# Norms on the tokens' partitions: sums of squares and the spreading of roots by transposes instead of fp32 products

## The chip, the core and the metric

The program runs on one core of a Trainium2 chip. A core has a matrix engine (TensorE, in the profile PE, with its weight loads as PEld), a vector engine (VectorE, DVE), an activation engine (ScalarE, ACT), a general engine (GpSimd, POOL) and a queue engine for transfers (SyncE, SP). Each engine has its own queue and takes its instructions in order; semaphores let one wait for another. SBUF and PSUM have 128 partitions; TensorE writes to PSUM only. A matrix instruction takes a stationary operand (128 x up to 128, loaded first) and a moving one, and gives stationary transposed times moving.

The metric is the time of one execution on the device in microseconds, as the median of several runs.

## The reference, cut to what matters

A two-layer encoder step: layer 0 is a state-space (SSD) mixer and a gated feed-forward net, layer 1 is banded attention and a second feed-forward net. There are 1088 tokens (1024 of a prompt, 64 of a running stream) of width 1024. Every part is wrapped in norms:

```python
def rmsnorm(x, w):
    xf = x.astype(jnp.float32)
    y = xf * lax.rsqrt(jnp.mean(xf * xf, axis=-1, keepdims=True) + EPS)
    return (y * w.astype(jnp.float32)).astype(x.dtype)
...
        xp = xp + rmsnorm(mp, nw[1])
        xp = xp + rmsnorm(swiglu(rmsnorm(xp, nw[2]), ffn_w_in[layer], ffn_w_out[layer]), nw[3])
```

and the SSD mixer has a gated norm of its own over four groups of 512 columns:

```python
    y = y.reshape(b, L, D_INNER) * jax.nn.silu(z.astype(jnp.float32))
    yg = y.reshape(b, L, SSM_GROUPS, D_INNER // SSM_GROUPS)
    yg = yg * lax.rsqrt(jnp.mean(yg * yg, axis=-1, keepdims=True) + EPS)
```

What matters here: per token one sum of squares over the features, one reciprocal root, and a product of every feature with that root.

## The kernel before, in words

**Layout.** Activations lie transposed: features on the partitions, tokens along the free axis. A token's sum of squares therefore runs over partitions and over feature tiles. Tokens come in three slices of 384, 384 and 320 (`SL`), or in four quarters of 256, 256, 288 and 288 (`QS`).

**A norm.** `add_sq` (lines 475 to 481) squares feature tiles on ScalarE and adds them up on GpSimd or VectorE into a tile `ssum` of 128 partitions by tokens. `rstd` (483) takes the sum over partitions: for each block of 128 tokens TensorE multiplies the block of `ssum` (stationary) with a column of ones (line 489), so a block's 128 sums arrive as one column of a PSUM tile `nst`, tokens on the partitions. Nine small VectorE operations (493 to 504) turn up to three such columns into reciprocal roots, one factor short: the constant `RL` is left for later. `diag` (506) makes, on VectorE, a diagonal matrix of the roots out of the identity, and `bcast` (513) multiplies a full matrix `frac`, all of whose entries are `RL`, with it on TensorE (516): the result, in a PSUM tile `nbp`, has on every partition the row of all tokens' roots. ScalarE copies it to SBUF (520), and VectorE uses it as a row factor.

**Where norms stand.** `rb_steps` (523) strings these together for the three norms at the start (`start_norm`), the two norms of each quarter after each mixer (`chain`, both layers), the end norm of each slice after each feed-forward net (`end`), and the scale for keys and values (also in `end`). The very last norm, of slice 2 in layer 1, has a second sum `more` with the squares of the last feature tile. The SSD stage calls `rstd` alone, once for each of four groups and three slices (`ssd_task`, line 931), and keeps the roots in `rst`; `build_y` (584) later spreads them, 16 times, and scales y with them on its way from DRAM to the output projection.

**Products.** The large products run as three reduced-precision products of high and low parts (lines 455 to 457, 1271 to 1273, 1470 to 1472); the products of the norms are full fp32 ones. Transposes through TensorE with the identity are in use elsewhere, as for B (799), x (830) and the attention weights (1715).

**Order.** TensorE's order is written out by hand: the program is one long run of large products, and side work (norms, SSD blocks, attention blocks) is held in generators. A counter `st.t` estimates TensorE's time; a generator yields `cost, delay, condition`, and is resumed at the next pump once the counter has moved on by the delay and the condition holds. So `RB_WAIT`, `CHW` and the other tables of delays say how much later on TensorE's queue a broadcast stands than the sums it needs. The order on the other engines is made by a planner at build time from priorities (`tc.high_priority`) and from when tiles come free. Two PSUM buffers (`ax`) are shared by `nst`, `nbp` and the small products and transposes of the side work; the ring `DG` holds two diagonals at most, and `DG.free` is a condition for the next one. Weights and scratch data come in on SP's queue.

Of the kernel before, what the change touches and what calls it, by code (L numbers as in the profile page):

```python
# [8 lines left out]
F32 = mybir.dt.float32  # L9
F32R = mybir.dt.float32r  # L10
I32 = mybir.dt.int32
AF = mybir.ActivationFunctionType
# [42 lines left out]
RWP = 3000, 0, 0  # L55

KBUF = 5
DGB = 2
RAWB, HLB, SGB = 2, 3, 5
NR, NRX = 16, 13  # L60

# [312 lines left out]
def hybrid_kernel(  # L374
# [21 lines left out]
    make_identity(nc, ident)  # L396
    ones = cp.tile([P, P], F32, name="ones")
    G.memset(ones, 1.0)
    frac = cp.tile([P, P], F32, name="frac")
    G.memset(frac, RL)  # L400
    pcs = cp.tile([P, NPC], F32, name="pcs")
    A.activation(ones[:, 0:1], ones[:, 0:1], AF.Square)

# [19 lines left out]
    W.tc, W.lent = tc, Lent(RX)  # L423
    W.raws.append(W.lent)
    UC = Cells(384, (R, 99))
    DG = Ring(nsb, "dg", DGB, [P, 3, P])

    def v4(t, n):
        return t[:, :4 * n].rearrange("p (k n) -> p k n", k=4)
# [52 lines left out]

    def rstd(ssum, inv, r, nb, more=None):

        sp, ts = ax("nst"), [ssum] if more is None else [ssum, more]
        for j, t in enumerate(ts):
            for i in range(nb):
                c = 4 * j + i
                PE.matmul(sp[:, c:c + 1], t[:, i * P:(i + 1) * P], ones[:, 0:1], start=True, stop=True)
        with tc.high_priority(HIP):  # L490
            v = nsb.tile([P, 12], F32, tag="nv", bufs=2, name="nv")
            a, h, y = v[:, 0:nb], v[:, 4:4 + nb], v[:, 8:8 + nb]
            V.tensor_scalar(a, sp[:, :nb], inv, EPS, op0=ALU.mult, op1=ALU.add)
            if more is not None:
                V.scalar_tensor_tensor(a, sp[:, 4:4 + nb], inv, a, op0=ALU.mult, op1=ALU.add)
            V.tensor_scalar(y.bitcast(I32), a.bitcast(I32), -0.5, float(0x5F3759DF), op0=ALU.mult, op1=ALU.add)


            V.tensor_tensor(h, y, y, op=ALU.mult)
            V.tensor_tensor(h, h, a, op=ALU.mult)  # L500
            V.scalar_tensor_tensor(a, h, RP[0], h, op0=ALU.add, op1=ALU.mult)
            V.scalar_tensor_tensor(a, a, RP[1], h, op0=ALU.add, op1=ALU.mult)
            V.scalar_tensor_tensor(a, a, RP[2], h, op0=ALU.add, op1=ALU.mult)
            V.scalar_tensor_tensor(r, a, RP[3], y, op0=ALU.add, op1=ALU.mult)

    def diag(r3, nb):
        dg = DG.get()
        V.tensor_tensor(
            dg[:, :nb], ident.unsqueeze(1).to_broadcast([P, nb, P]), r3.unsqueeze(2).to_broadcast([P, nb, P]), op=ALU.mult
        )  # L510
        return dg

    def bcast(dg, a, n, rb=None):

        bp = ax("nbp")
        PE.matmul(bp[:, :n], frac, dg.rearrange("p a b -> p (a b)")[:, a:a + n], start=True, stop=True)
        DG.put()
        if rb is None:
            rb = nsb.tile([P, 384], F32, tag="rb", bufs=1, name="rb")
        A.copy(rb[:, :n], bp[:, :n])  # L520
        return rb[:, :n]

    def rb_steps(ssum, n, out, wait=None, rb=None, more=None):

        nb = (n + P - 1) // P
        nr = nsb.tile([P, 4], F32, tag="nr", bufs=2, name="nr")
        rstd(ssum, 1.0 / D, nr[:, :nb], nb, more)
        yield 0.2, 0, DG.free
        with tc.high_priority(HIP):
            dg = diag(nr[:, :nb], nb)  # L530
        yield 0.1, wait or RB_WAIT
        with tc.high_priority(HIP):
            out.append(bcast(dg, 0, n, rb))
        yield 0.5, 0

    def apply_split(src, rb, wcol, n, dh, dl, eng=0):
        f = nsb.tile([P, 384], F32, tag="sq", bufs=2, name="uf")
# [46 lines left out]
    def build_y():  # L584

        for q, half in ((0, 0), (1, 0), (0, 1), (1, 1), (2, 0), (3, 0), (2, 1), (3, 1)):
            o, n = QS[q]
            got = []
            c0, c1, a = ((0, 2, 0), (2, 4, 0), (4, 7, 0), (6, 9, 32))[q]
            for kh in range(2):  # L590
                g = 2 * half + kh
                yield 0, 0, lambda: R.free(2) and DG.free() and all((g, s) in rst_done for s in ((0,), (0, 1), (1, 2), (2,))[q])
                h, l_ = rr(v4(R.get(), n)), rr(v4(R.get(), n))
                dg = diag(rst[:, c0:c1, g], c1 - c0)
                yield 0, 4.0
                rb = bcast(dg, a, n)
                with tc.high_priority(BYP[q]):
                    for k in range(4):
                        t_ = stage[0]()[:, :n]
                        nc.sync.dma_start(t_, yd_[:, 4 * g + k, o:o + n])  # L600
                        V.scalar_tensor_tensor(t_, t_, col(C_GN + 4 * g + k), rb, op0=ALU.mult, op1=ALU.mult)
                        A.copy(h[:, k, :], t_)
                        V.tensor_tensor(l_[:, k, :], t_, h[:, k, :], op=ALU.subtract)
                        got.append((h[:, k, :], l_[:, k, :]))
                yield 0.5, 0
            uy[half][q] = got
# [705 lines left out]
    def back(layer, start, cpost, xsrc, xmid, cpre, cpost2, xout, rb_out, done2):  # L1312
# [3 lines left out]
        with ExitStack() as es:  # L1316
# [30 lines left out]
            def end(s, y, ss, more=None):  # L1347

                o, n = SL[s]
                if s not in xss:  # L1350
                    yield from end_load(s)
                xs, xc = xss.pop(s)
                out = []
                if s == 2 and more is None:
                    yield 0, EP_W[2]
                steps = rb_steps(ss, n, out, ER_W[s], more=more)
                if more is not None:

                    xps = {}

                    def hold(ms):
                        for m in ms:
                            xps[m] = mm("xp") if m > 3 else px.tile([P, 512], F32, tag="mm", name="xp")
                            PE.matmul(xps[m][:, :n], ident, xs[m][0], start=True, stop=False)

                    yield next(steps)
                    hold(range(4))
                    yield next(steps)
                    yield next(steps)
                    hold((4, 5))  # L1370
                    for m in range(KD):
                        ym = y[:, m, :n]
                        V.scalar_tensor_tensor(ym, ym, col(cpost2 + m), out[0], op0=ALU.mult, op1=ALU.mult)
                        if m in xps:
                            PE.matmul(xps[m][:, :n], ident, ym, start=False, stop=True)
                            A.copy(ym, xps[m][:, :n])
                        else:
                            V.tensor_tensor(ym, ym, xs[m][0], op=ALU.add)
                        nc.sync.dma_start(xout[:, m, o:o + n], ym)
                    for c in xs:  # L1380
                        xc.put(c)
                    yr.put()
                    return
                yield from steps
                for m in range(KD):
                    ym = y[:, m, :n]
                    with tc.high_priority(ENP[s]):
                        V.scalar_tensor_tensor(ym, ym, col(cpost2 + m), out[0], op0=ALU.mult, op1=ALU.mult)
                        V.tensor_tensor(ym, ym, xs[m][0], op=ALU.add)
                        if m % 2:  # L1390
                            nc.sync.dma_start(xout[:, m - 1:m + 1, o:o + n], y[:, m - 1:m + 1, :n])
                    yield 0, ES[s]
                for c in xs:
                    xc.put(c)
# [598 lines left out]
```

## Time and profile before

| | |
|---|---|
| time of three runs | 3015.92, 3015.95, 3016.99 us; median 3015.95 |
| span of the profiled execution, first to last instruction | 3019.2 us; the page gives no other time for it |
| granted TensorE clock, mean | 0.995 |
| instructions | 56662 |
| moved by DMA | 335.43 MB, mean 111 GB/s |

In the profile, a group line gives the line of the kernel, the engine, the operation, output and inputs by the program's names, shapes, count, busy time and mean duration, then the engine's idle time before it and what ended it. A timeline line gives start and duration in us, and in brackets the idle time before it and what ended that. Durations of TensorE instructions overlap, since they are pipelined: what one costs the queue is the distance from start to start. A window line gives the stretch, the busy time of each engine, the granted TensorE clock and the DMA's share and rate.

### The profile page before, as it was taken

Reading aid. Unit: us, or ns where it says so; the run is one execution under the profiler, and the core shown is the slowest. Engines: PE = TensorE matmul, PEld = TensorE weight load, DVE = VectorE, ACT = ScalarE, POOL = GpSimd, SP = SyncE. Lnnn points to the kernel's source line nnn. Section 1 sums busy time; section 2 is a strip of 40 time slices with the busy share of each in tenths; the row PEclk is TensorE's granted clock in tenths of the full one; section 3 lists DMA queues with packets and bytes.
Section 4 is the critical chain, followed back from the end, with each engine's and each line's share of the span. In section 5 each row is a group of like instructions: output and inputs, shape, how many; then the busy total and the mean of one; then the engine's idle time right before and its main releaser. Section 6 shows DMA issues by size and latency. Waiting matters only on the chain.

```text
span 3019.2 us, 56662 instructions
## 1 busy us (share of the span) xinstructions
PE 2971.5 (98%) x21803; PEld 2907.2 (96%) x21803; DVE 2047.7 (68%) x4517; ACT 1462.0 (48%) x2643; POOL 699.4 (23%) x849
## 2 busy tenths in 40 slices
PE   8999999999999999999999999999999999999999
PEld 7999999998999999999999899999999999999998
DVE  7778877785768545575546878777768655475544
ACT  6756566564443322244444666555653322244443
POOL 1333333330121334351101000000131343452111
PEclk9999999999999999999999999999999999999999
DMA  3111111124555222245655322222356222245654
GB/s 120 34 58 52 59 48 51 60 67 139 182 143 157 74 80 75 80 151 179 200 168 164 96 81 79 70 64 84 118 173 180 74 77 81 79 146 176 212 177 135
DMA packets 180671, 335.43 MB, mean 111 GB/s; under 512 B 18192, under 2 KB 128400, under 8 KB 180400
## 3 DMA queue, kind: packets, MB, share of 16 engines
q1 hardware_dynamic: 178608, 325.45, 34.5%
q0 software_dynamic: 1792, 6.36, 1.1%
q8 instruction: 171, 2.80, 0.4%
q14 instruction: 100, 0.82, 0.1%
HBM read 264.69 MB, written 62.60 MB: 108 GB/s over the span
## 4 chain that ended last, share of the span: by engine, by line
PE 85%; DVE 8%; ACT 2%; DMA 2%; issue 2%; POOL 0%; SPq 0%; DVEq 0%; ACTq 0%; POOLq 0%
PE px L1271 9%; PE px L1272 9%; PE px L1273 9%; PE mm L455 7%; PE mm L457 7%; PE mm L456 7%; PE po L1470 6%; PE po L1471 6%; PE po L1472 6%; PE mmx L455 3%; PE mmx L456 3%; PE mmx L457 3%; PE po L1754 2%; PE ptp L1715 1%; PE yp L896 1%
## 5 line engine op out<-in xcount | busy, mean ns | idle before, releaser
L455 PE MATMUL mm<-r,hl 128*128 128x384 f32 (+2 forms) x1664 | 554.9, 333 | 8.6 <-DVE dt L705 4.1
L457 PE MATMUL mm<-r,hl 128*128 128x384 f32 (+2 forms) x1664 | 540.4, 325 | 1.6 <-DVE hl L352 0.9
L456 PE MATMUL mm<-r,hl 128*128 128x384 f32 (+2 forms) x1664 | 539.4, 324 | 0.0
L340 DVE TENSOR_TENSOR hl<-raw,hl 128x1024 fp32r<-128x1024 f32 (+1 forms) x219 | 263.0, 1201 | 222.1 <-ACT hl L339 219.3
L1272 PE MATMUL px<-r,hl 128*128 128x288 f32 (+1 forms) x1184 | 348.1, 294 | 0.0
L455 PEld LDWEIGHTS mm<-r,hl 128*128 128x128 f32 x1664 | 315.8, 190 | 11.8 <-ACT BT L782 4.3
L457 PEld LDWEIGHTS mm<-r,hl 128*128 128x128 f32 x1664 | 314.9, 189 | 3.3 <-DVE hl L352 2.3
L456 PEld LDWEIGHTS mm<-r,hl 128*128 128x128 f32 x1664 | 315.7, 190 | 0.5 <-issue 0.2
L1271 PE MATMUL px<-r,hl 128*128 128x288 f32 x1056 | 311.3, 295 | 0.0
L1273 PE MATMUL px<-r,hl 128*128 128x288 f32 x1056 | 311.3, 295 | 0.0
L339 ACT CAST hl<-raw 128x1024 fp32r<-128x1024 f32 (+1 forms) x219 | 219.1, 1005 | 179.5 <-PE po L1472 102.9
L481 POOL TENSOR_TENSOR ssum<-ssum,sq 128x256 f32<-128x256 f32 (+3 forms) x97 | 128.0, 1320 | 656.3 <-ACT sq L480 643.1
L1272 PEld LDWEIGHTS px<-r,hl 128*128 128x128 f32 x1184 | 222.7, 188 | 0.0
L1273 PE MATMUL px<-rx,hl 128*128 128x256 f32 x768 | 215.9, 281 | 5.1 <-DVE hl L340 5.1
L1271 PE MATMUL px<-rx,hl 128*128 128x256 f32 x768 | 216.5, 282 | 0.7 <-ACT hl L339 0.7
L1471 PE MATMUL po<-rx,hl 128*128 128x384 f32 (+1 forms) x624 | 202.0, 324 | 0.4 <-DVE rx L1335 0.3
L1470 PE MATMUL po<-rx,hl 128*128 128x384 f32 (+1 forms) x608 | 198.6, 327 | 0.6 <-ACT rx L1334 0.6
L1271 PEld LDWEIGHTS px<-r,hl 128*128 128x128 f32 x1056 | 198.6, 188 | 0.4 <-DVE u L1286 0.3
L1273 PEld LDWEIGHTS px<-r,hl 128*128 128x128 f32 x1056 | 198.6, 188 | 0.0
L1472 PE MATMUL po<-rx,hl 128*128 128x384 f32 (+1 forms) x608 | 196.9, 324 | 0.0
L1272 PE MATMUL px<-rx,hl 128*128 128x256 f32 x640 | 179.6, 281 | 0.0
L289 POOL TENSOR_TENSOR tt<-raw 128x512 f32<-128x512 f32 x40 | 54.8, 1369 | 449.5 <-DMA raw<-in_w_f_dram 311.6
(364 smaller groups left out, 8197.6 us busy)
## 6 DMA issues: line engine op xcount, KB each, us to landing
raw<-in_w_f_dram SPq DMA_DIRECT2D x154, 512.0 KB, 3.7
rx<-in_w_f_dram SPq DMA_DIRECT2D x54, 512.0 KB, 3.7
raw<-in_w_in_dram SPq DMA_DIRECT2D x40, 512.0 KB, 3.6
sg<-hscr SPq DMA_DIRECT2D x88, 192.0 KB, 3.6
raw<-in_w_f_dram SPq DMA_DIRECT2D x44, 384.0 KB, 3.3
raw<-in_w_so_dram SPq DMA_DIRECT2D x32, 512.0 KB, 3.8
raw<-in_w_kv_dram SPq DMA_DIRECT2D x18, 512.0 KB, 3.6
raw<-in_w_o_dram SPq DMA_DIRECT2D x16, 512.0 KB, 3.7
```

The costliest lines, as they stand in the source:

```text
L339: self.nc.scalar.copy(h, v)
L340: (eng or self.eng or self.nc.vector).tensor_tensor(lo, v, h, op=ALU.subtract)
L455: PE.matmul(ps[:, :n], h_, xh, start=(first and i == 0), stop=False)
L456: PE.matmul(ps[:, :n], h_, xl, start=False, stop=False)
L457: PE.matmul(ps[:, :n], l_, xh, start=False, stop=(last and i == nk - 1))
L481: (eng or G).tensor_tensor(ssum[:, :n], ssum[:, :n], q[:, :n], op=ALU.add)
L1271: PE.matmul(ps, wh, ah[:, k, :], start=(k == 0), stop=False)
L1272: PE.matmul(ps, wh, al[:, k, :], start=False, stop=False)
L1273: PE.matmul(ps, wl, ah[:, k, :], start=False, stop=(k == 3))
L1470: PE.matmul(ps[:, :n], wh, xh, start=(k == 0), stop=False)
L1471: PE.matmul(ps[:, :n], wh, xl, start=False, stop=False)
L1472: PE.matmul(ps[:, :n], wl, xh, start=False, stop=(k == FT - 1))
```

## The change

The sums of squares: where there is one sum tile (all norms but the last), each block of 128 tokens of `ssum` is transposed with the identity into `nst`, and VectorE sums the 128 columns of each block (`tensor_reduce`), then scales by the mean's factor. The last norm keeps its products.

The spreading: `diag`, its ring and `frac` go. `bcast` takes the column of roots of a block, repeated 128 times, as the stationary operand of a transpose with the identity; the result has the block's roots as a row on every partition. The factor `RL` moves to the scale of ScalarE's copy. For `build_y` the transposes cover whole blocks from the first one on, and the copy takes the wanted columns.

The delays: `rb_steps` has two yields instead of three (costs 0.3 and 0.35 in place of 0.2, 0.1 and 0.5) and no condition on a diagonal; `build_y` waits 2.5 in place of 4.0 before its broadcast; the end of the last slice is written for two yields.

```diff
-    frac = cp.tile([P, P], F32, name="frac")
-    G.memset(frac, RL)
...
-    DG = Ring(nsb, "dg", DGB, [P, 3, P])
...
-        sp, ts = ax("nst"), [ssum] if more is None else [ssum, more]
-        for j, t in enumerate(ts):
+        sp = ax("nst")
+        if more is None:
             for i in range(nb):
-                c = 4 * j + i
-                PE.matmul(sp[:, c:c + 1], t[:, i * P:(i + 1) * P], ones[:, 0:1], start=True, stop=True)
+                PE.transpose(sp[:, i * P:(i + 1) * P], ssum[:, i * P:(i + 1) * P], ident)
+        else:
+            for j, t in enumerate((ssum, more)):
+                for i in range(nb):
+                    c = 4 * j + i
+                    PE.matmul(sp[:, c:c + 1], t[:, i * P:(i + 1) * P], ones[:, 0:1], start=True, stop=True)
...
-            V.tensor_scalar(a, sp[:, :nb], inv, EPS, op0=ALU.mult, op1=ALU.add)
-            if more is not None:
+            if more is None:
+                sums = sp[:, :nb * P].rearrange("p (a b) -> p a b", b=P)
+                V.tensor_reduce(a, sums, axis=mybir.AxisListType.X, op=ALU.add)
+                V.tensor_scalar(a, a, inv, EPS, op0=ALU.mult, op1=ALU.add)
+            else:
+                V.tensor_scalar(a, sp[:, :nb], inv, EPS, op0=ALU.mult, op1=ALU.add)
...
-    def diag(r3, nb):
-        dg = DG.get()
-        V.tensor_tensor(
-            dg[:, :nb], ident.unsqueeze(1).to_broadcast([P, nb, P]), r3.unsqueeze(2).to_broadcast([P, nb, P]), op=ALU.mult
-        )
-        return dg
-
-    def bcast(dg, a, n, rb=None):
+    def bcast(r, a, n, rb=None):
 
         bp = ax("nbp")
-        PE.matmul(bp[:, :n], frac, dg.rearrange("p a b -> p (a b)")[:, a:a + n], start=True, stop=True)
-        DG.put()
+        for i in range((a + n + P - 1) // P):
+            PE.transpose(bp[:, i * P:(i + 1) * P], r[:, i:i + 1].to_broadcast([P, P]), ident)
...
-        A.copy(rb[:, :n], bp[:, :n])
+        A.activation(rb[:, :n], bp[:, a:a + n], AF.Copy, scale=RL)
...
-        yield 0.2, 0, DG.free
+        yield 0.3, wait or RB_WAIT
         with tc.high_priority(HIP):
-            dg = diag(nr[:, :nb], nb)
-        yield 0.1, wait or RB_WAIT
-        with tc.high_priority(HIP):
-            out.append(bcast(dg, 0, n, rb))
-        yield 0.5, 0
+            out.append(bcast(nr, 0, n, rb))
+        yield 0.35, 0
...
-                dg = diag(rst[:, c0:c1, g], c1 - c0)
-                yield 0, 4.0
-                rb = bcast(dg, a, n)
+                yield 0, 2.5
+                rb = bcast(rst[:, c0:c1, g], a, n)
...
-                    yield next(steps)
+                    got = next(steps)
                     hold(range(4))
-                    yield next(steps)
+                    yield got
                     yield next(steps)
```

More of the change, by code (lines that the diff above doesn't have):

```diff
@@ L57 @@
 KBUF = 5
-DGB = 2
 RAWB, HLB, SGB = 2, 3, 5
@@ L591, in build_y @@
                 g = 2 * half + kh
-                yield 0, 0, lambda: R.free(2) and DG.free() and all((g, s) in rst_done for s in ((0,), (0, 1), (1, 2), (2,))[q])
+                yield 0, 0, lambda: R.free(2) and all((g, s) in rst_done for s in ((0,), (0, 1), (1, 2), (2,))[q])
                 h, l_ = rr(v4(R.get(), n)), rr(v4(R.get(), n))
-                dg = diag(rst[:, c0:c1, g], c1 - c0)
-                yield 0, 4.0
-                rb = bcast(dg, a, n)
+                yield 0, 2.5
+                rb = bcast(rst[:, c0:c1, g], a, n)
                 with tc.high_priority(BYP[q]):
```

## The prediction

> **What bounds the kernel now.** I read the page first, then the windows, then the timeline around the norms.
>
> ```profile
> PE 2971.5 (98%) x21803; PEld 2907.2 (96%) x21803; DVE 2047.7 (68%) x4517; ACT 1462.0 (48%) x2643; POOL 699.4 (23%) x849
> ...
> PE 85%; DVE 8%; ACT 2%; DMA 2%; issue 2%; POOL 0%; SPq 0%; DVEq 0%; ACTq 0%; POOLq 0%
> ```
>
> TensorE (PE) is busy 98% of the span and the chain that ended last runs through it for 85%. That is an average, so two windows show the extremes (us; then busy time of PE, PEld, DVE, ACT, POOL; granted clock; DMA share; GB/s).
>
> ```profile
> 130.00:640.00 510.00, 509.92 (x3567) 494.54 (x3566) 408.93 (x1062) 313.12 (x491) 171.40 (x323) 1.00 0.17 53
> 640.00:705.00 65.00, 59.64 (x430) 56.47 (x429) 56.80 (x159) 39.05 (x76) 15.69 (x18) 0.97 0.33 101
> ```
>
> From 130 to 640 us (the SSD stage) PE has no idle time: a nanosecond saved on its queue is saved in the end. From 640 to 705 us, where the last SSD blocks, the gated y and the output projection meet, PE idles 5.4 us and VectorE (DVE) is busy 87%: there DVE decides. So I price PE's queue everywhere, then take off the places where PE waits for DVE anyway.
>
> **Sums of squares: products out, transposes in.** Which rows belong to the norms (instruction counts; ns minimum/median/maximum; first and last start):
>
> ```profile
> L489 PE MATMUL nst<-ones,ssum x158: 164/250/271, 21.4 to 3006.6; 128*128 128x1 f32 x158
> L489 PE MATMUL nst<-ones,ssg x72: 165/250/252, 229.0 to 690.7; 128*128 128x1 f32 x72
> L516 PE MATMUL nbp<-dg,frac x88: 377/405/799, 30.7 to 3009.7; 128*128 128x256 f32 x32, 128*128 128x288 f32 x32, 128*128 128x384 f32 x16, 128*128 128x320 f32 x8
> ```
>
> An fp32 product is two instructions: 230 are 115 products, in 40 norms; 88 are 44 broadcasts. Durations overlap, so what a group costs PE's queue is read from start to start:
>
> ```profile
> 899.57 0.28 PE L457 MATMUL mmx<-rx,hl 128*128 128x256 f32 x1
> 899.69 0.72 PE L489 MATMUL nst<-ones,ssum 128*128 128x1 f32 x6
> 900.27 0.36 PE L455 MATMUL mmx<-rx,hl 128*128 128x256 f32 x1
> ```
>
> ```profile
> 797.09 0.50 PE L489 MATMUL nst<-ones,ssum 128*128 128x1 f32 x4
> 797.45 0.38 PE L455 MATMUL mmx<-r,hx 128*128 128x288 f32 x1
> ```
>
> Three blocks take 0.58 us (900.27 less 899.69), two take 0.36. The replacement is in the kernel already, as the transposes of B into `bnp`: one instruction a block, since the three blocks show x3, not x6.
>
> ```profile
> 221.04 0.49 PE L799 MATMUL bnp<-ident,BT 128*128 128x128 f32 x3
> 221.29 0.42 PE L455 MATMUL mm<-r,hl 128*128 128x384 f32 x1
> ```
>
> Three transposes take 0.25 us. Two have no clean row; I take two thirds, 0.17, between 0.08 and 0.25. From the code, 31 norms have three blocks (3 at the start, 12 SSD groups, 8 of the chains, 5 ends, 3 for the K/V scale), 8 chain norms have two, and the last norm (the one with a second sum) keeps its products. Saved: 31 x (0.58 - 0.25) = 10.2 us and 8 x (0.36 - 0.17) = 1.5 us.
>
> **Broadcast: product out, transposes in.** The old cost by width:
>
> ```profile
> 1487.53 0.81 PE L516 MATMUL nbp<-dg,frac 128*128 128x384 f32 x2
> 1487.88 0.63 PE L1470 MATMUL po<-rx,hl 128*128 128x384 f32 x1
> ```
>
> ```profile
> 1652.59 0.70 PE L516 MATMUL nbp<-dg,frac 128*128 128x320 f32 x2
> 1652.89 0.57 PE L455 MATMUL mm<-r,hl 128*128 128x384 f32 x1
> ```
>
> ```profile
> 908.05 0.65 PE L516 MATMUL nbp<-dg,frac 128*128 128x288 f32 x2
> 908.32 0.50 PE L455 MATMUL mmx<-rx,hl 128*128 128x256 f32 x1
> ```
>
> ```profile
> 662.05 0.59 PE L516 MATMUL nbp<-dg,frac 128*128 128x256 f32 x2
> 662.29 0.52 PE L455 MATMUL mm<-r,hl 128*128 128x384 f32 x1
> ```
>
> Against 0.25 for three transposes (0.17 for two at width 256): 8 x 0.10 (384) + 4 x 0.05 (320) + 16 x 0.02 (288) + 16 x 0.07 (256) = 2.4 us. Together PE's queue gets 14.1 us shorter. If two blocks cost 0.25 or 0.08, the 24 two-block groups move this by about 2 us either way. The stationary operand here is one column repeated 128 times, which no transpose of the trace has. The nearest loads:
>
> ```profile
> L830 PEld LDWEIGHTS xtp<-ident,xsT 128*128 128x128 f32 x144 | 17.7, 141 | 0.7 <-POOL xsT L783 0.2
> L847 PEld LDWEIGHTS bcp<-acr,sel 128*128 128x128 f32 x96 | 14.8, 191 | 4.2 <-ACT ea L856 4.2
> ```
>
> `sel` is a repeated column too, in a product, and loads in 191 ns against 141 for a transpose; products with plain weights load in 190, so the repetition looks free and I take no charge. The bound: 50 ns on each of 116 such transposes (16 x 2 + 28 x 3), 5.8 us. Below, no gain.
>
> **VectorE.** It loses `diag` and gains the sum. The sum has no row; the nearest is a PSUM read of the same size. The view of groups (busy us, mean ns):
>
> ```profile
> L508 DVE TENSOR_TENSOR dg<-ident,nr 128x384 f32<-128x384 f32 x20 | 11.2, 558 | 0.5
> L800 DVE COPY Bn<-bnp 128x384 f32<-128x384 f32 x12 | 6.6, 552 | 0.8 <-PE bnp L799 0.7
> ```
>
> I take 0.55 us, with 0.4 below (the scan alone, estimated as the 552 less the 160 of a three-element operation of the norm) and 1.1 above, twice the copy; at 1.1 the chains at the five norms where PE waits (two at 41, one each at 682, 1684 and 2238) would be 0.55 longer each, 2.7 us less gain. So at 0.55 a norm followed by its broadcast stays as long on DVE: 0.55 earlier, 0.56 less later. The scaling on ScalarE's copy costs nothing: the copy exists already, and only a factor is added. [...]
>
> **Where PE waits, and the rest of the sum.** Near 41-46 us two start norms share DVE and PE stands until their roots are there; near 682-700 DVE decides.
>
> ```profile
> 46.33 2.26 PE L516 MATMUL nbp<-dg,frac 128*128 128x384 f32 x4 [2.31 <-DVE nr L504]
> ```
>
> ```profile
> 682.09 1.47 PE L489 MATMUL nst<-ones,ssg 128*128 128x1 f32 x12 [1.33 <-DVE ssg L928]
> ...
> 682.93 0.16 DVE L493 TENSOR_SCALAR nv<-nst 128x3 f32<-128x3 f32 x1
> ```
>
> Lost there: two start norms and their broadcasts (0.9), the three norms at 682-690 and the six narrow broadcasts at 662-700 (1.4), and the broadcasts at 1653-1690 and 2221-2253 (0.4): 2.7 us. The norms of the last two places keep their saving, because the DVE chain starts when the shorter PE group ends and is no longer than before; the sum waits for PE where the scaling of the old sums did, so the same work queues behind it on DVE, only 0.55 us longer. In the 640-705 stage DVE drops six diagonals, first and last
>
> ```profile
> 663.07 0.41 DVE L508 TENSOR_TENSOR dg<-ident,rst 128x256 f32<-128x256 f32 x1
> ...
> 700.71 0.43 DVE L508 TENSOR_TENSOR dg<-ident,rst 128x256 f32<-128x256 f32 x1 [1.84 <-PE nbp L516]
> ```
>
> (6 x 0.42 = 2.5) and takes three sums (1.65): 0.9 us back. The tail has no cover at all:
>
> ```profile
> 3008.51 0.16 DVE L504 SCALAR_TENSOR_TENSOR nr<-nv 128x3 f32<-128x3 f32 x1
> 3008.70 0.56 DVE L508 TENSOR_TENSOR dg<-ident,nr 128x384 f32<-128x384 f32 x1
> 3009.32 0.81 PE L516 MATMUL nbp<-dg,frac 128*128 128x320 f32 x2 [0.16 <-DVE dg L508]
> 3010.16 0.43 ACT L520 COPY rb<-nbp 128x320 f32<-128x320 f32 x1 [4.14 <-PE nbp L516]
> ```
>
> PE fills the wait with the held residual products until about 3009.15, so the broadcast starts 0.2 earlier and takes 0.5 instead of 0.81: 0.5 us. Removing `frac` and its fill frees POOL at the start, hidden behind the first weight load of the chain (start, us), so nothing; uncovered it could only gain.
>
> ```profile
> 1.72 4.42 DMA raw<-in_w_in_dram
> ```
>
> The delay before the y broadcasts falls from 4.0 to 2.5 us and no longer waits for a diagonal slot; that moves their loads on SP's queue and their work on DVE and ScalarE earlier, and I price it at zero, covered by the next units of PE. If that cover is gone, it is the slower rival.
>
> Sum: 14.1 - 2.7 + 0.9 + 0.5 = 12.8 us, from the profiled 3019.2 to 3006.4. The profile's span lies 3.25 us above the median of the runs, and the page shows nothing around it; with the same difference the runs come to about 3003.
>
> **The rivals.**
>
> (a) Waits take the gain back: the order on DVE and ACT is made anew, and two new waits of 2 us come up, each followed by a half-clock stretch:
>
> ```profile
> 1576.00:2340.00 764.00, 747.12 (x5887) 718.22 (x5886) 580.00 (x1562) 432.59 (x970) 63.08 (x83) 1.00 0.37 111
> 22.90:26.30 3.40, 3.40 (x12) 3.40 (x11) 3.40 (x16) 3.40 (x9) 0.00 (x0) 0.50 0.76 259
> ```
>
> After the wait for the first norm the clock is 0.50 for 3.4 us, a loss of 1.7. So 2 x 3.7 = 7.4 us: 3010. For it: the staging region is tight. Against: most broadcasts find their roots done well before.
>
> (b) Slower: the y broadcasts come 1.5 us earlier into the two shared PSUM buffers, which ScalarE empties late.
>
> ```profile
> 666.27 0.37 ACT L520 COPY rb<-nbp 128x256 f32<-128x256 f32 x1
> ```
>
> That copy came 4.2 us after the product of 662.05. If PE stands 1.5 us at each of the 16, that is 24 us against 12.8: 3027. It decides from nine of the sixteen on. Against it: only the first few copies come so late.
>
> (c) The repeated column loads slowly: 5.8 us given back, 3009. Against it, the 191 ns above.
>
> (d) More: the staging stage also sheds its half-clock stretch (1.7) and most of its 5.4 us of idle time; with 4 of these, 5.7 us more: 2997.
>
> [...]
>
> (f) That it doesn't do what it says (a transpose run as two products) is excluded by the x3 above.
>
> **How the numbers follow.** Forecast 0.55, (a) 0.12, (b) 0.08, (c) 0.10, (d) 0.10, (e) 0.05. What a measurement tells from no change is 0.2%, 6 us, so faster means under 3009.9: the forecast, (c), (d), (e) and a third of (a), 0.84; same: the rest of (a), 0.08; slower: (b), 0.08. The forecast's own range is 2999 to 3008 (two-block cost 2, sum on DVE 2.7). The whole range, 2995 to 3011, takes in (a), (c), (d) and (e) and leaves out (b).
>
> **What would show it.** The new groups in `nst` take 0.25 us from start to start, three instructions; the sum on DVE is near 0.55; no `dg` remains; the window from 130 to 640 us is shorter by 9 norms x 0.33 = 3.0 us; from `nr` to the last copy the tail loses 0.5. Wrong would be: PE idle in front of `nbp` or behind it in 660-850 us, more rows at clock 0.50, loads of the repeated column near 190 ns with starts further apart than 0.11, or a sum of 1 us on DVE.

## The result and the profile after

The changed kernel takes 2995.5 us (median of five runs, 2992.31 to 2998.83) against 3016.03 (five runs, 3015.92 to 3016.99): ratio 0.9931, 95% interval 0.9919 to 0.9943, 20.5 us less. The forecast was 3003, a gain of 12.8; the time stands 0.5 us inside the lower edge of the whole range of 2995 to 3011, and below the forecast's own range of 2999 to 3008. The profiled execution has a span of 2995.6 us.

The page after, with the busy times and the chain of work that ended last:

```profile
PE 2948.2 (98%) x21722; PEld 2891.8 (97%) x21722; DVE 2044.8 (68%) x4512; ACT 1460.1 (49%) x2643; POOL 699.0 (23%) x848
...
PE 88%; DVE 7%; DMA 2%; ACT 2%; issue 1%; POOL 0%; SPq 0%; DVEq 0%; ACTq 0%; POOLq 0%
```

PE's busy time fell by 23.3 us (2971.5 less 2948.2), the span by 23.6. PE's idle time is the span less its busy time: 47.7 us before, 47.4 after. So what was gained is time in which PE works (stretches at half clock included, which are taken out further below), and the waits as a whole stayed what they were. (The spans differ by more than the medians because the profiled execution of before is a slow one of its kind: a run of the change takes 1.7 us more than its span, and with the same 1.7 the profiled one of before lies 4.9 us above its median, that of after 1.8.)

The new groups, first by the tile `nst`, then by `nbp` (count, ns minimum/median/maximum, first and last start, shapes):

```profile
L484 PE MATMUL nst<-ident,ssum x73: 270/272/300, 21.2 to 2915.6; 128*128 128x128 f32 x73
L495 DVE TENSOR_REDUCE nv<-nst x39: 411/550/558, 22.0 to 2916.3; 128x3 f32<-128x384 f32 x31, 128x2 f32<-128x256 f32 x8
...
L484 PE MATMUL nst<-ident,ssg x36: 270/273/445, 226.4 to 686.3; 128*128 128x128 f32 x36
```

```profile
L514 PEld LDWEIGHTS nbp<-ident,nr x76: 132/135/138, 28.4 to 2986.2; 128*128 128x128 f32 x76
L514 PE MATMUL nbp<-ident,nr x76: 270/272/373, 28.6 to 2986.3; 128*128 128x128 f32 x76
L517 ACT ACTIVATE rb<-nbp x41: 362/406/494, 29.1 to 2986.6; 128x256 f32<-128x256 f32 x16, 128x288 f32<-128x288 f32 x16, 128x384 f32<-128x384 f32 x6, 128x320 f32<-128x320 f32 x3
```

There are 31 sums of three blocks and 8 of two, as counted from the code, and the sum takes 0.55 us. The repeated column loads in 135 ns, no slower than the 140 that the transposes of `ssum` take (the median of their loads in the same view): rival (c) is false. (The 76 transposes shown are those of the norms; the gated y has 40 more, with loads of 135 ns as well.)

**What a product costs.** The prediction took the cost from a group's start to the next start. The row after that one matters as well. The timeline of before, one row further than the prediction quoted it at 908 us:

```profile
908.32 0.50 PE L455 MATMUL mmx<-rx,hl 128*128 128x256 f32 x1
908.65 0.28 PE L456 MATMUL mmx<-rx,hl 128*128 128x256 f32 x1
908.77 0.28 PE L457 MATMUL mmx<-rx,hl 128*128 128x256 f32 x1
```

From one 256-wide product to the next there are 0.12 us, as between the last two rows; from 908.32 to 908.65 there are 0.33. The product behind the fp32 one starts early and is then held up 0.21 us itself. The broadcast of 908.05 cost 0.27 + 0.21 = 0.48 us, not 0.27. Read in this way over all places where PE had work on both sides, with a dozen products behind each so that nothing is left out, a broadcast product took 0.435 us at 256 columns, 0.48 at 288, 0.54 at 320 (one place only) and 0.64 at 384, about 1.6 ns a column (0.205 us for 128 more), where the reduced-precision product has 0.12 us for 256.

The same reading of what came in its place, in the timeline of after (three blocks, then two):

```profile
892.21 0.49 PE L484 MATMUL nst<-ident,ssum 128*128 128x128 f32 x3
892.46 0.37 PE L451 MATMUL mmx<-rx,hl 128*128 128x256 f32 x1
892.66 0.28 PE L452 MATMUL mmx<-rx,hl 128*128 128x256 f32 x1
```

```profile
795.57 0.38 PE L514 MATMUL nbp<-ident,nr 128*128 128x128 f32 x2
795.71 0.38 PE L451 MATMUL mmx<-r,hl 128*128 128x288 f32 x1
795.93 0.30 PE L452 MATMUL mmx<-r,hl 128*128 128x288 f32 x1
```

Three transposes: 0.25 us to the next start, 0.45 to the second; less 0.12 for the product between, 0.33. Two: 0.36 less 0.13 to 0.15, some 0.22. The old norms, read alike, took 0.675 us with three blocks and 0.44 with two; in before:

```profile
900.27 0.36 PE L455 MATMUL mmx<-rx,hl 128*128 128x256 f32 x1
900.47 0.28 PE L456 MATMUL mmx<-rx,hl 128*128 128x256 f32 x1
```

From 899.69 to 900.47, less 0.12, is 0.66. For the norms the two readings agree in the difference, since both old and new hold up the product behind by about 0.1: 0.34 us saved instead of 0.33. For the broadcasts they don't: the product hides 0.2 to 0.3 us behind the next start, the transposes 0.08. What is saved is then 31 x 0.34 + 8 x 0.23 = 12.4 us for the norms, and 16 x 0.215 (256) + 16 x 0.15 (288, three blocks) + 4 x 0.21 (320) + 8 x 0.31 (384) = 9.2 us for the broadcasts, in all 21.6.

The SSD stage, where PE's waits are the same in both kernels, is a clean test. The scan's product `yp`, before and then after:

```profile
L896 PE MATMUL yp<-dm,xd x576: 218/273/325, 100.3 to 671.8; 128*64 128x128 f32 x176, 128*64 128x64 f32 x16
```

```profile
L889 PE MATMUL yp<-dm,xd x576: 218/273/325, 97.7 to 665.8; 128*64 128x128 f32 x176, 128*64 128x64 f32 x16
```

571.5 us from first to last before, 568.1 after: 3.4 less, with nine norms (9 x 0.335 = 3.0) and the first two broadcasts of y (2 x 0.215 = 0.4) between.

**Half-clock stretches.** In the clock's records PE's clock falls to 0.50 for 3.4 us at a time, and each such stretch costs 1.7 us if PE has work all through it (an estimate: half of its length). Before they begin at 22.9, 46.8, 74.1, 691.9, 749.9, 971.8, 1572.5 and 2340.5 us; after at 44.2, 57.8, 71.5, 679.0, 955.5 (two on end), 1696.2, 1706.4 and 2317.4, with the start of one more at 2993.3. Two places show what went and what came. Around 750 and 1572 us, before and then after (stretch; length, busy PE, PEld, DVE, ACT, POOL; clock; DMA share; GB/s):

```profile
742.00:762.00 20.00, 18.52 (x132) 17.42 (x131) 17.44 (x33) 10.44 (x23) 5.56 (x4) 0.91 0.62 184
1560.00:1580.00 20.00, 19.06 (x119) 18.31 (x119) 13.52 (x33) 9.85 (x19) 1.34 (x1) 0.91 0.60 184
```

```profile
742.00:762.00 20.00, 20.00 (x174) 20.00 (x174) 14.52 (x28) 9.79 (x20) 7.39 (x6) 1.00 0.53 162
1560.00:1580.00 20.00, 20.00 (x140) 19.98 (x139) 16.01 (x26) 10.49 (x18) 4.51 (x2) 1.00 0.65 188
```

A stretch of half clock is gone in each. The windows show the same times and not the same work, which the change reaches 7 to 19 us earlier. Matched product by product, PE's waits around 750 us fell from 1.5 to 1.0 us only, since the change waits 0.54 us at 740.92 and 0.44 at 741.75; around 1570 us they fell from 0.9 to 0.1. In the attention stage the opposite; the timeline of after, with PE's idle time and its releaser in brackets:

```profile
1694.58 0.44 PE L453 MATMUL mm<-r,hl 128*128 128x384 f32 x1 [2.18 <-DVE hl L351]
...
1704.53 0.74 PE L1708 MATMUL ptp<-ident,sc 128*128 128x128 f32 x5 [1.93 <-DVE mx L1686]
```

In before the wait at the same weight split was 0.20 us (1716.63). From the last product ahead of these two waits that stands at the same place in PE's order to the first such one behind them (1671 to 1718 us), the change takes 5.2 us more than before. So the gain is 21.6 by the queue, and a few microseconds to and fro by waits and half-clock stretches. The experiments test the first and show how large the second is.

### The profile page after: what moved, and what is told of

It is laid out like the page before. It is cut to its first block, busy times and chain, and to the rows that moved or that the text cites. A ratio compares the mean times of both kernels' runs of the same rounds, so it can differ in the third digit from the quotient of the medians.

```text
span 2995.6 us, 56513 instructions
## 1 busy us (share of the span) xinstructions
PE 2948.2 (98%) x21722; PEld 2891.8 (97%) x21722; DVE 2044.8 (68%) x4512; ACT 1460.1 (49%) x2643; POOL 699.0 (23%) x848
## 4 chain that ended last, share of the span: by engine, by line
PE 88%; DVE 7%; DMA 2%; ACT 2%; issue 1%; POOL 0%; SPq 0%; DVEq 0%; ACTq 0%; POOLq 0%
PE px L1264 9%; PE px L1265 9%; PE px L1266 9%; PE mm L451 8%; PE mm L453 8%; PE mm L452 8%; PE po L1464 6%; PE po L1465 6%; PE po L1463 6%; PE mmx L452 3%; PE mmx L451 3%; PE mmx L453 3%; PE po L1747 2%; PE ptp L1708 1%; PE yp L889 1%
```

## The experiments

Each kernel ran five times (one of them four) beside nine runs of the kernel before on its chip; that stood at 3016.22 for the first four kernels, 3018.18 for the next three and 3019.64 for the last three, so kernels of different groups are compared by ratio. The theories are Q: the time follows PE's queue, with products priced in the second start behind them; P (later called S): the queue, as the prediction priced it; O: the shorter delays and the new order made the gain; V (later R): VectorE's relief from the diagonals made it. N and D come up for the last three kernels only, and are told in what was expected of those.

**One part alone: the sums.** Before, with only `rstd` changed; diagonals, broadcast products and delays stay.

```diff
-                PE.matmul(sp[:, c:c + 1], t[:, i * P:(i + 1) * P], ones[:, 0:1], start=True, stop=True)
+                PE.transpose(sp[:, i * P:(i + 1) * P], ssum[:, i * P:(i + 1) * P], ident)
...
+                V.tensor_reduce(a, sums, axis=mybir.AxisListType.X, op=ALU.add)
```

> Only the sums by transposes and a VectorE sum; diagonals, the product that spreads the roots, and all delays as before. Theory Q (the gain is TensorE's queue, and a product of a norm costs what it delays over the next dozen matmuls: 0.675 us for three blocks against 0.335 by transposes, 0.44 against 0.21 for two): 31 x 0.34 + 8 x 0.23 = 12.4 us, so 3002 to 3006. Theory O (the gain comes mainly from the new delays and the order they make): at most 6 us, 3010 or more.

3003.96 us (3001.94 to 3006.11), ratio 0.9958 [0.9945, 0.9972]: 12.3 us less, against 12.4 by the queue. VectorE has 13.7 us more to do (2061.4 busy against 2047.7), and that cost nothing that can be seen.

**The other part alone: the spreading.** The changed kernel, new delays included, with `rstd` of before.

```diff
-                PE.transpose(sp[:, i * P:(i + 1) * P], ssum[:, i * P:(i + 1) * P], ident)
+                PE.matmul(sp[:, c:c + 1], t[:, i * P:(i + 1) * P], ones[:, 0:1], start=True, stop=True)
...
-                V.tensor_reduce(a, sums, axis=mybir.AxisListType.X, op=ALU.add)
```

> Only the spreading by transposes, with the new delays; the sums by products as before. Theory Q, counted over the next dozen matmuls (0.435, 0.48, 0.54, 0.64 us for a product of width 256, 288, 320, 384; 0.22 or 0.33 for transposes): 9.2 us, so 3005 to 3009. Theory P (as the prediction had it, counted to the next start alone): 2.4 us and the tail's 0.5, so 3012 to 3014.

3006.44 us (3002.78 to 3008.68), ratio 0.9964 [0.9951, 0.9976]: 9.8 us less. The prediction's 2.4 us for this part is refuted, the 9.2 holds. The two parts add up to 22.1, the whole gave 20.5.

**The delays of before in the changed kernel.**

```diff
-        yield 0.3, wait or RB_WAIT
+        yield 0.2, 0
+        yield 0.1, wait or RB_WAIT
...
-        yield 0.35, 0
+        yield 0.5, 0
...
-                yield 0, 2.5
+                yield 0, 4.0
```

> The changed kernel with the delays of before (0.2, 0.1 and 0.5 in three yields; 4.0 in front of the y broadcasts). Theory Q: the instructions carry the gain, so within 5 us of the changed kernel, 2991 to 3001. Theory O: the delays carry it, so 3005 or more.

2995.15 us (2993.27 to 2998.57), ratio 0.9929 [0.9917, 0.9942]: the same as the change. The delays made none of the gain.

**The diagonals kept.** The changed kernel with all 44 diagonal products still made on VectorE, into a tile that nothing reads.

```diff
+        with tc.high_priority(HIP):
+            spare(nr[:, :nb], nb)
...
+                spare(rst[:, c0:c1, g], c1 - c0)
                 yield 0, 2.5
```

> The changed kernel with the 44 diagonal products put back on VectorE, into a tile that nobody reads. Theory V (VectorE's relief carries a good part of what came beyond the forecast): 5 us or more slower than the changed kernel, 3000 or more. Theory Q: TensorE's queue is unchanged, and only the staging stage (six diagonals, 2.5 us) and the tail (0.6) can feel it: 0 to 3 us, 2995 to 2999.

3003.25 us (2998.2 to 3005.49), ratio 0.9952 [0.994, 0.9965]: 7.7 us more than the change by the medians, 6.3 by the ratios, whose intervals just overlap; as V has it, and Q (2995 to 2999) has not. The timeline shows three waits of PE of over 1.2 us at places where the change does not wait at all:

```profile
846.49 0.40 PE L451 MATMUL mmx<-r,hl 128*128 128x288 f32 x1 [1.25 <-ACT r L604]
...
970.52 0.39 PE L1273 MATMUL px<-rx,half 128*128 128x256 f32 x1 [1.31 <-DVE p L1290]
...
1864.95 0.39 PE L1685 MATMUL S<-K,Qh 128*128 128x256 f32 x1 [1.91 <-DVE pT L1722]
```

PE's idle time is 54.8 us (3003.8 less 2949.0) against 47.4. Near 1865 us there is no norm at all, and the first of these waits stands in the kernel with the old delays too, which makes no diagonal:

```profile
843.75 0.40 PE L451 MATMUL mmx<-r,hl 128*128 128x288 f32 x1 [1.07 <-ACT r L596]
```

So another explanation is that the planner puts the other work in another order, whatever is added. PE's own order of all instructions outside the norms is the same as in the change; VectorE's, leaving out the diagonals, differs at 94 of 4471 places. Two kernels split the diagonals.

**Diagonals of the norms only; diagonals of the gated y only.** Each keeps one of the two additions of the last diff.

> The changed kernel with the 28 diagonal products of the norms kept on VectorE (15.6 us of its work, into a tile that nothing reads), none for the gated y. Theory R (the 7.7 us that all 44 cost are VectorE's work, in proportion): 2.3 times the share of the y diagonals, 2999.5 to 3002.5. Theory O (the 7.7 us come with a new order and its few stalls, not with the work): this kernel and the one with the y diagonals do not stand in the ratio 15.6 to 6.7, and what is lost stands at one to three stalls of over 1 us, some of them where no norm is near.

> The changed kernel with the 16 diagonal products of the gated y kept on VectorE (6.7 us of its work), none for the norms. Theory R: 2996.5 to 2999.5, and less than the kernel with the diagonals of the norms by about 3. Theory O: it stands alone at up to the whole 7.7 us or at nothing, with the difference at one to three stalls.

Norms: 2999.07 us (2996.97 to 3003.47), ratio 0.9936 [0.9924, 0.9949]. y: 2996.93 (2991.88 to 2998.6), ratio 0.9928 [0.9915, 0.9942]. By the ratios to their own runs of before neither can be told from the change (0.9931). Both together (0.9952) stand above either, though the intervals of the norms' kernel and of the one with all 44 overlap. By the absolute times R's ranges were all but met (2999.07 against 2999.5 to 3002.5, 2996.93 inside its own), but these runs of before were 2.0 us slower than those of the kernel with all 44. Of the 19.1 us less than before with the norms' diagonals and 21.2 with y's, each is within 1.4 us of the 20.5 of the change, so R is not supported.

The traces say where the loss is. Matched product by product with the change, the kernel with all 44 takes 3.8 us more from 836 to 850 us (the first of the three waits and a half-clock stretch behind it), 1.6 from 965 to 980 and 2.2 from 1850 to 1870: 7.6 of the 8.2 us between the two spans, at the three stalls. Neither of the kernels with a part of the diagonals loses more than 0.4 us at any of these places. That is O's picture. Which instruction's place in VectorE's order made the stalls was not followed, and 1 to 2 us for the diagonals themselves can't be excluded.

**The price itself, doubled.** Before, with each broadcast product issued twice.

```diff
-        PE.matmul(bp[:, :n], frac, dg.rearrange("p a b -> p (a b)")[:, a:a + n], start=True, stop=True)
+        for _ in range(2):
+            PE.matmul(bp[:, :n], frac, dg.rearrange("p a b -> p (a b)")[:, a:a + n], start=True, stop=True)
```

> The kernel before, with each of the 44 broadcast products issued twice into the same buffer, the second over the first. Theory Q (a product costs TensorE's queue what its columns take, read in the start of the second matmul behind it: 0.435 us at 256 columns, 0.48 at 288, 0.54 at 320, 0.64 at 384): 16 x 0.435 + 16 x 0.48 + 4 x 0.54 + 8 x 0.64 = 21.9 us, so 3034 to 3041. Theory S (the prediction's reading, from the product's start to the next start: 0.24, 0.27, 0.30, 0.35): 12.2 us, so 3025 to 3031.

3030.38 us (3028.65 to 3032.7), ratio 1.004 [1.0028, 1.0053]: 12.2 us more, which is S to the tenth, and 9.7 short of Q's 21.9. Yet the timeline of this kernel shows Q's price:

```profile
907.86 1.13 PE L517 MATMUL nbp<-dg,frac 128*128 128x288 f32 x4
908.61 0.49 PE L455 MATMUL mmx<-rx,hl 128*128 128x256 f32 x1
908.94 0.28 PE L456 MATMUL mmx<-rx,hl 128*128 128x256 f32 x1
```

From 907.86 to 908.94, less 0.12, there are 0.96 us for two products, twice 0.48; at 384 columns it is 1.29, twice the 0.64. By S it would be 0.75 here (0.48 and a further 0.27). The page of this kernel shows where the rest went:

```profile
PE 2985.2 (99%) x21891; PEld 2917.5 (96%) x21891; DVE 2045.4 (68%) x4517; ACT 1463.1 (48%) x2643; POOL 697.4 (23%) x849
```

With a span of 3026.9 PE is idle 41.7 us, 6.0 less than before: some products stand where PE waited anyway. And it has three half-clock stretches within the span instead of eight, 8.5 us less.

Two stretches of the program settle the price, since PE neither waits nor loses clock there in any of these kernels. PE's order outside the norms is the same in all of them up to 1670 us, so each window runs from one product to the same product of the other kernel. The first holds ten broadcasts (four of 256 columns, six of 288) and four sums of two blocks; before, products twice, spreading only, sums only, change:

```profile
764.99:852.02 87.03, 87.03 (x664) 86.18 (x663) 65.22 (x143) 39.78 (x76) 10.89 (x13) 1.00 0.53 164
```

```profile
760.73:852.37 91.64, 91.64 (x684) 89.95 (x683) 66.80 (x143) 40.89 (x77) 11.51 (x13) 1.00 0.51 156
```

```profile
756.45:841.47 85.02, 85.02 (x670) 85.02 (x669) 61.60 (x133) 39.50 (x76) 11.39 (x13) 1.00 0.54 164
```

```profile
757.32:843.47 86.15, 86.15 (x656) 85.25 (x655) 66.79 (x147) 39.88 (x76) 10.90 (x13) 1.00 0.55 166
```

```profile
754.97:839.06 84.09, 84.09 (x663) 84.09 (x662) 63.08 (x137) 39.66 (x76) 11.46 (x13) 1.00 0.53 166
```

The doubled products take 4.61 us more (4 x 0.435 + 6 x 0.48 = 4.6 by Q, 4 x 0.24 + 6 x 0.27 = 2.6 by S). The spreading saves 2.01 (1.8 by Q, 0.4 by S), the sums save 0.88 (0.9 by Q, 0.8 by S), and the change saves 2.94 (2.7 and 1.2).

The second stretch, from 1580.12 to 1640.17 us in before, holds three broadcasts of 384 columns and one sum of three blocks. The doubled products take 1.93 us more there (1.9 by Q, 1.05 by S), the spreading saves 0.93 (0.9 and 0.3), and the change saves 1.28 (1.3 and 0.6). So the price of Q is what a product costs the queue in these two stretches, where it never waits.

For the whole program waits and clock have to be taken off. The table does this for every kernel: idle time is the span less PE's busy time, the loss is half the length of the stretches at 0.50 inside the span, and the rest is PE's own work at full clock.

| kernel | span | PE idle | half-clock loss | rest | rest against before |
|---|---|---|---|---|---|
| before | 3019.2 | 47.7 | 13.7 | 2957.8 | |
| change | 2995.6 | 47.4 | 16.5 | 2931.7 | -26.1 |
| sums only | 3000.6 | 46.3 | 8.5 | 2945.8 | -12.0 |
| spreading only | 3002.0 | 47.0 | 8.9 | 2946.1 | -11.7 |
| delays of before | 2993.8 | 47.9 | 11.0 | 2934.9 | -22.9 |
| diagonals kept | 3003.8 | 54.8 | 11.9 | 2937.1 | -20.7 |
| diagonals of the norms | 2997.3 | 50.8 | 12.5 | 2934.0 | -23.8 |
| diagonals of y | 2990.2 | 47.2 | 8.5 | 2934.5 | -23.3 |
| products twice | 3026.9 | 41.7 | 5.1 | 2980.1 | +22.3 |
| only the y delay of before | 2996.4 | 47.5 | 14.5 | 2934.4 | -23.4 |
| only the norm delays of before | 2991.2 | 47.8 | 9.7 | 2933.7 | -24.1 |
| change, again | 2996.4 | 47.7 | 16.5 | 2932.2 | -25.6 |

The rest of the doubled kernel moved by 22.3 us, where Q has 21.9; sums only by 12.0, where it has 12.4. For the change and for the spreading it is 4.5 and 2.5 us more than the 21.6 and 9.2 of the queue. The kernels whose queue is the change's own stand between -20.7 and -26.1, so the split itself is good to some 3 us. A part of that is counted twice: where PE also stood idle in a half-clock stretch, the table takes that time off as idle and half of it again as loss. In the change that is 3.3 us of idle time, mostly at its very end, and without it the -26.1 is -24.6. What else scatters was not traced. The time of a kernel is this rest, which the queue predicts so far, plus idle time and half-clock loss, which no price of an instruction gives, and which lie anywhere between 46.8 us (products twice) and 66.7 (diagonals kept). S fits the doubled kernel's time because the waits and the clock happened to give back what it leaves out. The runs say the same as the traces: the mean granted clock was 0.9970 in the five runs of the doubled kernel and 0.9957 in the nine beside them, which is 9.1 against 13.1 us of loss (an estimate: one minus the clock, times the span). The 12.2 us of the medians, these 4.0 and the 6.0 of idle time make 22.2.

**The two stalls of the attention stage, and a version below both.** The delays one by one, beside the unaltered change: first with only the y delay of before (4.0), then with only the norm delays of before (the first two hunks of the diff above).

> The changed kernel with only the y delay of before (4.0 instead of 2.5). Theory N (the delays only choose among orders that are worth the same): within 3 us of the changed kernel in the same comparison, TensorE's busy time less the waits within 3 us of its, and only the places of the waits differ. Theory D (the norm delays 0.3 and 0.35 make the two stalls of about 2 us at 1692 and 1702 us, each with a half-clock stretch): the stalls stay here, and the kernel is no faster than the changed one.

> The changed kernel with the norm delays of before (0.2, 0.1 and 0.5 with its extra step) and the y delay of the change (2.5). Theory D: the stalls at 1692 and 1702 us and their two half-clock stretches are gone and none comes in their place, so 4 to 7 us faster than the changed kernel in the same comparison, a version that beats both. Theory N: within 3 us of it.

> The changed kernel once more, unaltered, on the chip of the other two, as their yardstick. Both theories: a ratio to the kernel before of 0.992 to 0.994, with the median within 2 us of 2995.5 after the kernel before is set to 3016.

Only the y delay: 2998.2 us (2997.08 to 2999.63), ratio 0.9932 [0.9919, 0.9944]. Only the norm delays: 2994.15 (four runs, 2992.86 to 2995.39), ratio 0.9918 [0.9905, 0.9932]. The change again: 2996.78 (2995.85 to 2998.22), ratio 0.9926 [0.9912, 0.9939]; times 3016 that is 2993.7, so both parts of its expectation were met.

The window of the two stalls, in the change and then with the norm delays of before, followed by the timeline of the latter at the weight split:

```profile
1690.00:1712.00 22.00, 17.54 (x125) 16.14 (x125) 15.93 (x52) 12.90 (x31) 0.00 (x0) 0.84 0.17 48
```

```profile
1690.00:1712.00 22.00, 19.27 (x157) 16.64 (x155) 18.55 (x60) 14.14 (x32) 0.00 (x0) 1.00 0.17 51
```

```profile
1693.85 0.44 PE L453 MATMUL mm<-r,hl 128*128 128x384 f32 x1 [0.20 <-DVE hl L351]
```

The wait is 0.20 us again, as in before, and the clock 1.00; the stalls of 2.18 and 1.93 us stand unchanged in the kernel with only the y delay and in the repeat. PE's order shows the cause. Outside the norms it is the same as before in each kernel with the norm delays of before. In each kernel with the new ones 143 of its 21485 instructions stand at another place, all of them between 1670 and 1704 us of the change. So D is right about the cause: the new norm delays make the order that has these stalls. Between the last product ahead of the moved ones and the first behind (1671 to 1718 us) the order of before is worth 5.2 us against the profiled change, 4.8 against its repeat. PE's idle time as a whole did not fall (47.8 us against 47.7 in the repeat): the order of before has waits of its own, as 1.31 us at 1669 and 1.54 at 2222. The span of the profiled execution is 5.2 us shorter than that of the repeat, the median 2.6, less than D's 4 to 7 and inside N's 3. The runs of the two kernels do not overlap, though the intervals of their ratios do: a small gain, and by median and ratio the fastest version here.

## Why the prediction was right or wrong

**Direction and mechanism: right.** PE's queue bounds the kernel, and the transposes shorten it; waits and VectorE did not take the gain. PE's idle time is the same to 0.3 us. That the time still falls into the whole range is luck as far as the sum goes: the range reaches down to 2995 for rival (d), and what brought the time there was a term of the sum.

**The step that failed: "Against 0.25 for three transposes (0.17 for two at width 256) ... = 2.4 us".** The cost of the broadcast products was read from their start to the next start (0.24 to 0.35 us). They take 0.435 to 0.64, and the spreading is worth 9.2 us by the queue and 9.8 in the medians. The prediction's own rows carried the hint: the product behind the broadcast has a duration of 0.50 instead of 0.28, and the broadcast itself 0.65. The error of 7 us is nearly all of the 7.7 by which the gain was missed: with 9.2 and 12.4 in its place the sum would be 20.3. That it comes so near the 20.5 is better than the split deserves, which is good to some 3 us, and half-clock stretches cost 2.8 us more in the profiled change than in the profiled one of before.

**Norms, 10.2 + 1.5: right**, 12.4 by the queue and 12.3 measured alone. The SSD stage got 3.0 us shorter for nine norms, as forecast.

**The places where PE waits, -2.7, and the staging stage, +0.9.** Not seen as a total, since idle time did not grow. At one site it is there: near 682 us PE now waits 3.21 us for the gated sums instead of 1.33.

```profile
678.29 0.55 PE L484 MATMUL nst<-ident,ssg 128*128 128x128 f32 x3 [3.21 <-DVE ssg L921]
```

Matched product by product, the stage from 640 to 705 us does 2.5 us less work and waits 1.5 us longer, so it got 1.05 us shorter. By the prediction it would be 0.9 (1.4 of work, less 1.4, and 0.9 back): near in sum, but both the work saved and the wait are larger than its terms. At 41 us and from 2160 to 2300 us nothing was lost, since PE waits there at most 0.1 us longer than before; near 1690 us the two new stalls hide whatever was.

**The sum on VectorE, 0.55: right**, 550 ns for three blocks: no longer than the 552 ns copy of the same size out of PSUM in before. The factor on ScalarE's copy, priced at nothing, cost 8 ns there: the median of the 41 copies into `rb` is 406 ns, before 398.

**The tail, 0.5: right.** In the timeline of after:

```profile
2985.56 0.16 DVE L508 SCALAR_TENSOR_TENSOR nr<-nv 128x3 f32<-128x3 f32 x1
...
2986.05 0.49 PE L514 MATMUL nbp<-ident,nr 128*128 128x128 f32 x3
...
2986.57 0.44 ACT L517 ACTIVATE rb<-nbp 128x320 f32<-128x320 f32 x1 [3.51 <-PE nbp L514]
```

From `nr` to the end of the copy 1.45 us, before 2.08 (3008.51 to 3010.59): 0.6 less.

**The rivals.** (a) came true in its mechanism, two new waits of 2 us each followed by a half-clock stretch, at 1694 and 1704 us, not in the staging region to which the prediction pointed; they took 5.2 us, but other waits and stretches went. What brought them was the order of PE's own instructions, which the new norm delays changed, and not the order on VectorE and ScalarE. (b) did not come: between 700 and 850 us PE waits twice, for 0.54 and 0.44 us, both times for scaled rows of y, as for 0.86 us in before (748.34), and the y delay alone moved the median by 1.4 us. (c) is false by the loads of 135 ns. (d) did not come where it said: the stretch of the staging stage is still there, at 679.0 instead of 691.9. Stretches of its kind went at 750 and 1572 us instead, and as many came at 1696 and 1706. (e), with its chance of 0.05, stands for a half-clock stretch more at 41 and at 682 us, and that term no run shows: near each place there is one in the change, at 44.2 and 679.0, as there is one in before, at 46.8 and 691.9. Of the signs of being wrong that the prediction names, one came: more rows at clock 0.50, nine and the start of a tenth instead of eight. Each of them follows a wait, but for the second of the two on end and the one at 57.8 us, which is told of below.

## What to carry to other kernels

The price of a matmul in a busy queue is read in the second start behind it, or over a dozen instructions, against the same stretch without it: the next start alone hides what the next instruction pays (0.27 us in place of 0.48 for the broadcast at 908 us). The work on this queue, 98% busy, is then forecast well by such prices (to 0.4 us for the doubled products and for the sums alone, to 4.5 for the change), and the time with an uncertainty of 5 to 10 us here, from a handful of waits and half-clock stretches that move with the order. When a kernel's time contradicts a price (as with the doubled product), compare stretches in which the engine neither waits nor loses clock, and split the rest into work, idle time and clock loss, before the price is given up. Such a stretch also tests a price when the run as a whole can't.

## What the hardware showed besides

**The half-clock stretches lie on a grid in these traces.** Within the trace of before, and within that of the change, the starts of these stretches are whole multiples of 3.4133 us apart, to within 0.03 us over 2318 and 2949 us. With each of the two traces cut into such steps, from where its clock records begin (5.8 and 6.7 us), all eight steps at full clock in which PE stood idle for more than 2.0 us were followed by half clock; of the eleven with 1.3 to 2.0 us of idle time seven were, and of those with less two, told of at the end. In the kernel with the diagonals of y a wait of 2.19 us that is shared between two steps, with 1.17 and 1.03 us of idle time, passed without one. The first of the two stalls by such steps in the change, then that wait:

```profile
1692.77:1696.18 3.41, 1.60 (x8) 1.32 (x9) 3.23 (x13) 3.40 (x11) 0.00 (x0) 1.00 0.21 50
1696.18:1699.60 3.42, 3.42 (x16) 3.42 (x15) 1.81 (x5) 0.87 (x2) 0.00 (x0) 0.50 0.05 5
```

```profile
1687.15:1690.56 3.41, 2.24 (x15) 1.92 (x13) 3.12 (x11) 3.11 (x8) 0.00 (x0) 1.00 0.16 45
1690.56:1693.97 3.41, 2.38 (x15) 2.10 (x16) 3.28 (x13) 2.81 (x9) 0.00 (x0) 1.00 0.11 27
1693.97:1697.39 3.42, 3.42 (x25) 3.42 (x24) 1.54 (x3) 0.97 (x2) 0.00 (x0) 1.00 0.41 120
```

```profile
1691.59 0.45 PE L453 MATMUL mm<-r,hl 128*128 128x384 f32 x1 [2.19 <-DVE hl L351]
```

In the first PE is busy 1.60 of 3.41 us and the next step runs at 0.50; in the second the wait ends at 1691.59, is shared between two steps with 2.24 and 2.38 us busy, and the clock stays at 1.00. So the same wait cost 2.2 or, with half of a stretch of 3.41 us added, 3.9 us (an estimate) by where it fell. With up to nine such steps in a kernel this may be what spreads the runs of the change over 6.5 us; that was not shown run by run. The granted clocks of the runs go that way: of the nine runs of before beside the last three kernels the three below 3017 us had 0.996 to 0.997, the four above 3020 us 0.994 to 0.995.

**Two stretches have little or no wait before them.** In the change one begins at 57.8 us, behind a step in which PE is busy all the time (3.41 of 3.41 us), 2.1 us of it with eighteen narrow products:

```profile
55.13 2.19 PE L686 MATMUL dtn<-stk,dtT 64*128 64x32 f32 x18
```

That at 1572.5 us in before follows a step with 0.4 us of idle time. What triggers these two was not shown; the narrow products were not tried by themselves.
